# Seven products for eight: Strassen's scheme in the input projection of a short convolution

## The chip, the core and the metric

The kernel runs on one core of a Trainium2 chip. The core has a matrix engine (TensorE, PE in the profile; the loading of its stationary operand is listed apart as PEld), a vector engine (VectorE, DVE), a scalar engine (ScalarE, ACT), GpSimd (POOL) and SyncE (SP), which here issues the transfers between device memory and SBUF, the on-chip memory. PE writes into PSUM, eight banks of 128 x 512 f32. The metric is the device time of one execution in microseconds, as the median of several runs.

## The reference

The model is a trunk of four layers over x (1024 tokens x 1024 channels, f32), with mixers of three kinds: layers 0 and 3 a gated short convolution, layer 1 a diagonal state-space layer, layer 2 an RWKV-7 layer. The change concerns layer 3:

```python
def short_conv_mixer(x, w_in, conv_k, w_out):
    bg, cg, h, z = jnp.split(x @ w_in, 4, axis=-1)
    u = cg * h
    conv = ...                    # width 3 over the tokens, per channel
    return (bg * conv * jax.nn.silu(z)) @ w_out
...
    r = DN_ALPHA * x + y
    r = r + (p[i] @ ple_proj[i]) * jax.nn.sigmoid(r @ ple_gate[i])
    x = layer_norm(r, ln_g[i], ln_b[i])
```

The input projection x @ w_in is 1024 x 1024 x 4096; in the code its four parts have the numbers i = 0 (bg), 1 (cg), 2 (h) and 3 (z).

## The kernel before

Activations lie transposed in SBUF: channels on the 128 partitions, in 8 blocks, tokens along the free dimension in two halves h of 512. For precision every f32 operand is split into a high part, cast by ACT, and a low part, the remainder, subtracted on DVE (`split_into`, L191, for 128 x 512; `wload`, L285 and L286, for a weight block of 128 x 1024, loaded by SP at L282). A product of one output block (128 channels, one half of the tokens) over the 1024 input channels is `mm3`: 8 terms k, each with three matmuls of 512 columns (high x high at L308, high x low at L309, low x high at L310), so 24 matmuls into one PSUM bank.

In the last layer's mixer (`conv_layer`, `unit_both`) the units m = 0 to 7 run over blocks of output channels. Each takes four weight blocks, in the order i = 1, 2, 3, 0, and makes four products per half: cg (copied by ACT), h (u = h x cg, then the three taps of the convolution on DVE), z (its sigmoid on ACT, products on DVE and POOL), and b (the last product, then the split into y). Units 0 and 1 first run for the first half of the tokens, then for the second, with their weights loaded twice, because the second half of x is still being normalised: `ln_gen` of the layer before is a generator, and its pieces are pulled in between the products (counts CP). It takes the mean (`mu`), subtracts it, sums the squares (POOL and DVE), forms 1/sqrt of the variance (`var`, a few small steps on 128 x 4), spreads it (`ln_y`) and scales and splits each block of x (L697, L705, L191). Units 2 to 7 use each weight for both halves. Then `w_out_rows` makes the output product, first for the first half, with the residual alpha x x taken from the high and low parts of x (two DVE steps), and `ple_ln_rows` the gate and the last LayerNorm.

Where buffers lie is set by tags: x in a0 and a1 (by half), y in b0 and b1. Temporaries come from seven slots (`tt`), weights from three buffers each of raw, high and low (wraw, wh, wl), products from four PSUM banks (pmm) and four more (paux). Weights are loaded up to two ahead (AHEAD). The framework orders the instructions of each engine at build time by program order and a model of their durations; on the chip each engine runs its own queue in that order and waits on semaphores.

## Time and profile before

| | |
|---|---|
| three runs | 2869.85, 2872.4, 2874.41 us (median 2872.4) |
| profiled execution | 2874.98 us, its span 2873.3 us |
| PE busy in the span | 2722.6 us (95%), 15131 matmuls |
| DVE, ACT, POOL busy | 1886.0 us (66%), 1121.9 us (39%), 635.8 us (22%) |
| last layer's input products | from 2288.0 to 2648 us |
| its output product | from 2649 to 2737 us |

Numbers of the trace are times from the start of the span. A group is listed by line of the code, engine, operation and tiles (out<-in). Matmuls overlap in their pipeline, so the step from one start to the next, and not the duration of one, tells what they cost. The 40 slices of the page are 71.8 us each.

### The profile page before, as it was taken

What the parts mean: (1) busy time and instruction counts of PE and PEld (TensorE: products, weight loads), DVE (VectorE), ACT (ScalarE), POOL (GpSimd) and SP (SyncE); (2) the same over time, 40 slices, a digit from 0 to 9 for tenths busy, and PEclk for the clock granted to TensorE, in tenths of its full rate; (3) what the DMA queues carried; (4) which work ended last, traced back from release to release, by engine and by line L of the source; (5) the groups of instructions that cost most, each with busy time, mean ns of one, the idle gap of its engine ahead of it and who ended that gap; (6) DMA issues with size and microseconds to landing.
All of it is one profiled execution on the core that took longest, in us unless ns stands there. A gap on an engine that the chain in (4) does not pass through costs nothing.

```text
span 2873.3 us, 40597 instructions
## 1 busy us (share of the span) xinstructions
PE 2722.6 (95%) x15131; PEld 2163.6 (75%) x15131; DVE 1886.0 (66%) x3428; ACT 1121.9 (39%) x2147; POOL 635.8 (22%) x690
## 2 busy tenths in 40 slices
PE   8999999999999999999888799898889999999998
PEld 6877788878877887577666577666667778888887
DVE  6787765477657347878788676887848473333654
ACT  3333322242144223655556465565534231112322
POOL 1243423221207033104333101333232210000000
PEclk9999999999999999999997799997899999999999
DMA  5333322358783333463222254222334332112320
GB/s 166 98 95 96 94 77 62 88 152 225 209 247 124 103 92 119 144 214 96 73 81 89 69 182 141 74 86 83 110 92 143 104 91 59 44 46 64 118 66 37
DMA packets 449749, 312.67 MB, mean 109 GB/s; under 512 B 48360, under 2 KB 393744, under 8 KB 449552
## 3 DMA queue, kind: packets, MB, share of 16 engines
q1 hardware_dynamic: 449552, 310.08, 36.0%
q8 instruction: 119, 1.95, 0.3%
q14 instruction: 78, 0.64, 0.1%
HBM read 240.28 MB, written 69.21 MB: 108 GB/s over the span
## 4 chain that ended last, share of the span: by engine, by line
PE 73%; DVE 14%; ACT 4%; issue 3%; POOL 2%; DMA 2%; SPq 0%; DVEq 0%; POOLq 0%; ACTq 0%
PE op L309 3%; PE op L308 3%; PE op L310 3%; PE gp L310 3%; PE zp L308 3%; PE gp L309 3%; PE zp L309 3%; PE zp L310 3%; PE gp L308 3%; PE sp L308 3%; PE sp L309 3%; PE sp L310 3%; DVE tv L1739 2%; PE hp L308 2%; PE hp L309 2%
## 5 line engine op out<-in xcount | busy, mean ns | idle before, releaser
L286 DVE TENSOR_TENSOR wl<-wraw,wh 128x1024 fp32r<-128x1024 f32 x283 | 365.9, 1294 | 311.5 <-ACT wh L285 303.5
L285 ACT CAST wh<-wraw 128x1024 fp32r<-128x1024 f32 x283 | 296.9, 1050 | 695.5 <-PE gp L309 191.8
L608 POOL TENSOR_TENSOR ln_s<-ln_s,rp 128x512 f32<-128x512 f32 x42 | 60.1, 1430 | 209.8 <-DVE rp L604 209.8
L1825 DVE SCALAR_TENSOR_TENSOR state<-state,pc,p 64x64 f32<-64x64 f32 x256 | 71.0, 277 | 50.1 <-PE p L1822 45.6
L1739 DVE TENSOR_TENSOR tv<-ti,mi 128x128 f32<-128x128 f32 (+3 forms) x128 | 97.1, 759 | 2.4
L1818 PE MATMUL p<-state,ra 128*128 128x128 f32 x256 | 65.7, 344 | 27.3 <-DVE state L1825 25.2
L1819 ACT COPY uv<-p 64x128 f32<-64x128 f32 x128 | 33.2, 259 | 138.8 <-PE p L1818 138.1
L1818 PEld LDWEIGHTS p<-state,ra 128*128 128x128 f32 x256 | 46.3, 219 | 52.7 <-DVE state L1825 42.1
L1673 PEld LDWEIGHTS s<-ra,kb 64*128 64x128 f32 x512 | 64.2, 212 | 20.4 <-ACT scr L1679 6.5
L1673 PE MATMUL s<-ra,kb 64*128 64x128 f32 x512 | 74.7, 314 | 4.4 <-ACT scr L1679 2.1
L1822 PE MATMUL p<-uv,kbt 128*128 128x128 f32 x256 | 67.7, 351 | 10.4 <-ACT uv L1819 10.3
L310 PE MATMUL gp<-r_0h,wl 128*128 128x512 f32 x192 | 76.9, 400 | 0.0
L308 PE MATMUL zp<-x_0h,wh 128*128 128x512 f32 x192 | 76.7, 400 | 0.0
L309 PE MATMUL gp<-r_0l,wh 128*128 128x512 f32 x192 | 76.7, 399 | 0.0
L308 PE MATMUL gp<-r_0h,wh 128*128 128x512 f32 x192 | 76.5, 398 | 0.0
L308 PE MATMUL gp<-r_1h,wh 128*128 128x512 f32 x192 | 76.4, 398 | 0.0
L310 PE MATMUL gp<-r_1h,wl 128*128 128x512 f32 x192 | 76.0, 396 | 0.1
L623 POOL TENSOR_TENSOR rp<-r_0h,r_0l 128x512 f32<-128x512 f32 x24 | 37.4, 1589 | 174.9 <-PE op L309 174.9
L308 PE MATMUL zp<-x_1h,wh 128*128 128x512 f32 x192 | 75.9, 396 | 0.0
L310 PE MATMUL zp<-x_1h,wl 128*128 128x512 f32 x192 | 75.8, 395 | 0.0
L309 PE MATMUL zp<-x_1l,wh 128*128 128x512 f32 x192 | 75.7, 394 | 0.0
L310 PE MATMUL zp<-x_0h,wl 128*128 128x512 f32 x192 | 75.7, 394 | 0.0
(740 smaller groups left out, 8437.6 us busy)
## 6 DMA issues: line engine op xcount, KB each, us to landing
wraw<-in_conv_w_in_dram SPq DMA_DIRECT2D x80, 512.0 KB
wraw<-in_rwkv_w_rkvz_dram SPq DMA_DIRECT2D x64, 512.0 KB
wraw<-in_ple_gate_dram SPq DMA_DIRECT2D x56, 512.0 KB
wraw<-in_conv_w_out_dram SPq DMA_DIRECT2D x24, 512.0 KB
wraw<-in_ssm_w_in_dram SPq DMA_DIRECT2D x21, 512.0 KB
xt<-xd SPq DMA_DIRECT2D x32, 256.0 KB
wraw<-in_rwkv_w_out_dram SPq DMA_DIRECT2D x16, 512.0 KB
wraw<-in_ple_proj_dram SPq DMA_DIRECT2D x14, 512.0 KB
```

The lines of the kernel that those rows point to most:

```text
L285: nc.scalar.copy(wh, raw)
L286: nc.vector.tensor_tensor(wl, raw, f32(wh[:]), ALU.subtract)
L308: nc.tensor.matmul(ps, lh, xh, start=(k == 0), stop=False)
L309: nc.tensor.matmul(ps, lh, xl, start=False, stop=False)
L310: nc.tensor.matmul(ps, ll, xh, start=False, stop=(k == kt - 1))
L608: nc.gpsimd.tensor_tensor(s, s, rs, ALU.add)
L623: (eng or nc.gpsimd).tensor_tensor(rs, f32(rh[:]), f32(rl[:]), ALU.add)
L1673: nc.tensor.matmul(pss[hd][:, c * P:(c + 1) * P], kb[rows, 2 * c + w, :], ra[rows, 2 * c + w, :], start=True, stop=True)
L1739: V.tensor_tensor(tv, ti[:, b:8, 4 * b:4 * b + 4].unsqueeze(2).to_broadcast([P, n, c, 4]), mi[:, 4 * b:4 * b + 4, 0:c].rearrange("p q c -> ...
L1818: nc.tensor.matmul(p1, R.ra[:, c, :], st, start=False, stop=False, skip_group_check=True)
L1822: last = nc.tensor.matmul(p2[:, 0:P], R.kbt[c // 4][:, c % 4, :], uv, start=True, stop=True)
L1825: V.scalar_tensor_tensor(st[cs, cs], st[cs, cs], R.pc[cs, c:c + 1], p2[cs, cs], ALU.mult, ALU.add)
```

## The change

Layer 3's input projection is done by Strassen's scheme in Winograd's form: output channels are taken in pairs of blocks (m, m + 4), tokens in the two halves, input channels in two halves of four blocks. For each of 16 quads (m = 0 to 3, i = 1, 2, 3, 0) seven products q = 1 to 7 of four terms (12 matmuls) take the place of eight. `x_quad` makes sums and differences of the four quarters of x, once for each k, and splits them, inside the generator `ln_gen` after the normalisation of the second half; `w_quad` loads the two weight blocks of a quad and makes and splits the sums of weights (c1, c3 and one in place in r1). Products that several outputs share are added up in PSUM, with DVE or ACT reading the bank in between (s2, s3), and in SBUF by DVE.

For m = 0, 1, 2 the products q1 and q2, which need only the first half of x, are made ahead (12 products, `lead`), while `ln_gen` is pulled (counts QX); q1 is kept in b0, or in memory for m = 2. `tail` puts q4 and q3 of a quad behind q6 of the next. The first tap of the convolution moves from DVE to ACT. Blocks of y with m other than 3 and 7 are stored to memory and loaded again and split before the output product. x in f32 is stored to memory by `ln_gen` and loaded again for the residual, which is then one DVE step. Tags change: y in a0 and b1, sums of x in a1, b0 and b1, r in a1 and a0. The terms of the output product run in the order 0, 1, 2, 4, 5, 6, 3, 7 (ks).

```diff
         for idx, l in enumerate(layers):
             last = idx == len(layers) - 1
             nxt = None if last else layers[idx + 1] % 3
+            S.quads = idx > 0 and (layers[-1] % 3 == 0) and (last or idx == len(layers) - 2)
+            if nxt == 0:
+                S.xf, S.X = [[None, None] for _ in range(NB)], {}
...
     for l in layers:
         kind, j, last = l % 3, l // 3, l == layers[-1]
-        if kind == 0:
+        if kind == 0 and last and l:
+            for m in range(NH):
+                for i in (1, 2, 3, 0):
+                    add("conv_w_in", (j,), i * D + m * P)
+            order.append(None)
+            for _ in range(2):
+                blocks("conv_w_out", (j,))
+            for c in range(2):
+                add("ple_proj", (l,), c * HT, 2, HT)
+        elif kind == 0:
...
+def w_fill(S):
+    while len(S.wready) < min(1 + AHEAD, len(S.worder)) and S.worder[len(S.wready)]:
+        S.wready.append(wload(S, S.worder[len(S.wready)]))
...
 def conv_layer(S, x, l, bg, prep, last):
     nc, A = S.nc, S.A
     region_b(S)
+    if S.quads:
+        return conv_quads(S, x, l, bg)
...
     if last:
-        w_out_rows(S, l, ("conv_w_out", (j,)), y, resid, "a")
+        w_out_rows(S, l, ("conv_w_out", (j,)), y, resid, ("a0", "a1"))
...
+NH = 3
+QX = 1, 2, 2, 3, 3, 2, 3, 3, 3, 3, 3, 3
+def x_quad(S, x, xf, k):
+    V = S.nc.vector
+    x11, x12, x21, x22 = xf[k][0], xf[k][1], xf[k + 4][0], xf[k + 4][1]
+    X = S.X
+    X[3, k] = slot_split(S, "a1", "b22")
+    split_into(S, X[3, k], x22)
+    V.tensor_tensor(x11, x11, x12, ALU.subtract)
+    yield
+    V.tensor_tensor(x12, x22, x12, ALU.subtract)
+    V.scalar_tensor_tensor(x22, x11, -1.0, x22, ALU.mult, ALU.subtract)
+    yield
+    t4 = tt(S, "t4") if k == 3 else x21
+    V.scalar_tensor_tensor(t4, x22, -1.0, x21, ALU.mult, ALU.subtract)
+    for q, t in ((6, x22), (5, x11), (7, x12), (4, t4)):
+        X[q, k] = slot_split(S, ("a1", "b0", "b1", "b1")[k], f"t{q}")
+        split_into(S, X[q, k], t)
+        if q in (5, 4):
+            yield
+def w_quad(S, name, idx, c0, full):
+    nc = S.nc
+    V = nc.vector
+    W = S.A[name][idx].rearrange("(k p) n -> p k n", p=P)
+    r0, r1 = (S.wp.tile([P, NB, P], F32, tag="wraw", name="wraw", bufs=3) for _ in range(2))
+    nc.sync.dma_start(r1, W[:, :, c0 + HT:c0 + HT + P])
+    nc.sync.dma_start(r0, W[:, :, c0:c0 + P])
+    yield
+    q = {}
+    def hilo(src, k=NB):
+        if k == NB:
+            wh, wl = (S.wp.tile([P, k, P], F32R, tag=t, name=t, bufs=3) for t in ("wh", "wl"))
+        else:
+            wh, wl = (S.ws.tile([P, k, P], F32R, tag=t, name=t, bufs=1) for t in ("w3h", "w3l"))
+        nc.scalar.copy(wh, src)
+        V.tensor_tensor(wl, src, f32(wh[:]), ALU.subtract)
+        return wh, wl
+    if full:
+        w = hilo(r0)
+        q[1], q[2] = (*w, 0), (*w, 4)
+        yield
+    c1 = S.ws.tile([P, NB, P], F32, tag="c1", name="c1", bufs=1)
+    V.tensor_tensor(c1[:, 4:8, :], r1[:, 0:4, :], r1[:, 4:8, :], ALU.add)
+    V.tensor_tensor(c1[:, 0:4, :], c1[:, 4:8, :], r0[:, 0:4, :], ALU.add)
+    yield
+    w = hilo(c1)
+    q[6], q[5] = (*w, 0), (*w, 4)
+    yield
+    c3 = S.ws.tile([P, 4, P], F32, tag="c3", name="c3", bufs=1)
+    V.tensor_tensor(c3, r0[:, 0:4, :], r1[:, 0:4, :], ALU.add)
+    V.tensor_tensor(r1[:, 0:4, :], c1[:, 0:4, :], r0[:, 4:8, :], ALU.add)
+    yield
+    w = hilo(c3, 4)
+    q[7] = (*w, 0)
+    yield
+    w = hilo(r1)
+    q[3], q[4] = (*w, 0), (*w, 4)
+    S.wq.append(q)
+    yield
+def conv_quads(S, x, l, bg):
+    nc, A = S.nc, S.A
+    V, G, SC = nc.vector, nc.gpsimd, nc.scalar
+    j = l // 3
+    kw = [S.vec[("conv_k", j, t)] for t in range(3)]
+    X = S.X
+    y = [[None, None] for _ in range(NB)]
+    yd = [S.dram.tile([P, T], F32, tag=f"yd{m}", name=f"yd{m}") for m in range(NB)]
+    s1d = [S.dram.tile([P, HT], F32, tag=f"s1d{i}", name=f"s1d{i}") for i in range(4)]
+    carry, cgs, cvs = {}, {}, {}
+    half = lambda h: slice(h * HT, (h + 1) * HT)
+    st = ExitStack()
+    S.ws = st.enter_context(S.tc.tile_pool(name="ws", bufs=1))
+    S.wq = []
+    tq = lambda nm: S.ws.tile([P, HT], F32, tag="q", name=nm, bufs=4)
+    def mms(ps, w, q, first):
+        wh, wl, k0 = w
+        for k in range(4):
+            xh, xl = X[q, k]
+            nc.tensor.matmul(ps, wh[:, k0 + k, :], xh, start=first and k == 0, stop=False, skip_group_check=True)
+            nc.tensor.matmul(ps, wh[:, k0 + k, :], xl, start=False, stop=False, skip_group_check=True)
+            nc.tensor.matmul(ps, wl[:, k0 + k, :], xh, start=False, stop=k == 3, skip_group_check=True)
+    def block(ps, base=None):
+        if base is None:
+            return ps
+        V.tensor_tensor(base, base, ps, ALU.add)
+        return base
+    def use(i, m, h, v):
+        if i == 1:
+            if v.space == PSUM:
+                t = tq("cg")
+                SC.copy(t, v)
+                v = t
+            cgs[m, h] = v
+        elif i == 2:
+            u = S.tmp.tile([P, HT + 2], F32, tag="t_u", name="u")
+            if h == 0:
+                G.memset(u[:, 0:2], 0.0)
+            else:
+                G.tensor_copy(u[:, 0:2], carry.pop(m))
+            V.tensor_tensor(u[:, 2:], v, cgs.pop((m, h)), ALU.mult)
+            if h == 0:
+                carry[m] = S.tmp.tile([P, 2], F32, tag="t_car", name="car", bufs=4)
+                G.tensor_copy(carry[m], u[:, HT:HT + 2])
+            cv = cvs[m, h] = tt(S, "cv")
+            SC.activation(cv, u[:, 0:HT], AF.Copy, scale=kw[0][:, m:m + 1])
+            V.scalar_tensor_tensor(cv, u[:, 1:HT + 1], kw[1][:, m:m + 1], cv, ALU.mult, ALU.add)
+            V.scalar_tensor_tensor(cv, u[:, 2:HT + 2], kw[2][:, m:m + 1], cv, ALU.mult, ALU.add)
+        elif i == 3:
+            sg = S.tmp.tile([P, HT], F32, tag="ln_v" if h else "ln_s", name="sg", bufs=1) if not bg else tt(S, "sg")
+            SC.activation(sg, v, AF.Sigmoid, scale=1.0 if m < 4 else -1.0)
+            V.tensor_tensor(sg, v, sg, ALU.mult)
+            G.tensor_tensor(cvs[m, h], cvs[m, h], sg, ALU.mult)
+        else:
+            cv = cvs.pop((m, h))
+            V.tensor_tensor(cv, v, cv, ALU.mult)
+            if m % 4 == 3:
+                y[m][h] = slot_split(S, ("a0", "b1")[h], f"y{m}_{h}")
+                split_into(S, y[m][h], cv)
+            else:
+                nc.sync.dma_start(yd[m][:, half(h)], cv)
+    ahead = [(m, i) for m in range(NH) for i in (1, 2, 3, 0)]
+    quads = [(m, i) for m in range(4) for i in (1, 2, 3, 0)]
+    wg = [None] * (len(quads) + 1)
+    def w_begin(p):
+        if p < len(quads):
+            m, i = quads[p]
+            wg[p] = w_quad(S, "conv_w_in", (j,), i * D + m * P, m >= NH)
+            next(wg[p])
+    def w_step(p, n=1):
+        for _ in range(n):
+            if wg[p] is not None and next(wg[p], None) is None:
+                pass
+    s1 = {}
+    for k in range(4):
+        X[1, k], X[2, k] = x[k][0], x[k + 4][0]
+    def lead(n):
+        m, i = ahead[n]
+        w = wprep(S, "conv_w_in", (j,), i * D + m * P)
+        ps = S.pmm.tile([P, HT], F32, tag="mm", name="q1")
+        mms(ps, (*w, 0), 1, True)
+        s = tt(S, "s1d") if m == 2 else slot(S, "b0", "s1")
+        SC.copy(s, ps)
+        if m == 2:
+            nc.sync.dma_start(s1d[n % 4], s)
+        else:
+            s1[m, i] = s
+        return w, ps
+    cur = lead(0)
+    na = len(ahead)
+    for n, (m, i) in enumerate(ahead):
+        nxt = lead(n + 1) if n + 1 < na else None
+        w, ps = cur
+        pull(bg, QX[n])
+        mms(ps, (*w, 4), 2, False)
+        use(i, m, 0, block(ps))
+        cur = nxt
+        if n == na - 5:
+            w_begin(0)
+        if n >= na - 4:
+            w_step(0, 2)
+    while bg:
+        pull(bg)
+    for _ in wg[0]:
+        pass
+    w_begin(1)
+    def tail(st8):
+        (m, i), q, A_, C_, base, s2, v22 = st8
+        mms(A_, q[4], 4, False)
+        use(i, m + 4, 0, block(A_, base))
+        if i == 2:
+            use(i, m + 4, 1, v22)
+        mms(C_, q[3], 3, False)
+        use(i, m, 1, block(C_, s2))
+    def load_y(m, h):
+        t = tt(S, "yl")
+        nc.sync.dma_start(t, yd[m][:, half(h)])
+        y[m][h] = slot_split(S, ("a0", "b1")[h], f"y{m}_{h}")
+        split_into(S, y[m][h], t)
+    prev = None
+    for p, (m, i) in enumerate(quads):
+        q = S.wq.pop(0)
+        final = p == len(quads) - 1
+        if m == 1 and NH == 3:
+            s1[2, i] = slot(S, "b0", "s1")
+            nc.sync.dma_start(s1[2, i], s1d[(1, 2, 3, 0).index(i)])
+        A_ = S.pmm.tile([P, HT], F32, tag="mm", name="qa")
+        if m < NH:
+            base = s1.pop((m, i))
+            mms(A_, q[6], 6, True)
+            s2 = tt(S, "s2")
+            V.tensor_tensor(s2, base, A_, ALU.add)
+            w_step(p + 1, 2)
+            if prev:
+                tail(prev)
+            w_step(p + 1)
+        else:
+            base = None
+            mms(A_, q[1], 1, True)
+            sq = slot(S, "b0", "s1")
+            SC.copy(sq, A_)
+            w_step(p + 1, 2)
+            if prev:
+                tail(prev)
+            D_ = S.paux.tile([P, HT], F32, tag="aux", name="qd")
+            mms(D_, q[2], 2, True)
+            use(i, m, 0, block(D_, sq))
+            w_step(p + 1)
+            if final:
+                for k in (0, 1, 2, 4, 5, 6):
+                    load_y(k, 0)
+            mms(A_, q[6], 6, False)
+            s2 = tt(S, "s2")
+            SC.copy(s2, A_)
+            w_step(p + 1)
+        C_ = S.pmm.tile([P, HT], F32, tag="mm", name="qc")
+        mms(C_, q[5], 5, True)
+        w_step(p + 1)
+        mms(A_, q[7], 7, False)
+        s3 = tq("s3")
+        if base is None:
+            SC.copy(s3, A_)
+        else:
+            V.tensor_tensor(s3, base, A_, ALU.add)
+        block(C_, s3)
+        if i != 2:
+            use(i, m + 4, 1, s3)
+        if wg[p + 1] is not None:
+            for _ in wg[p + 1]:
+                pass
+        w_begin(p + 2)
+        if final:
+            S.worder.pop(0)
+            w_fill(S)
+        prev = (m, i), q, A_, C_, base, s2, s3
+    tail(prev)
+    for k in (0, 1, 2, 4, 5, 6):
+        load_y(k, 1)
+    st.close()
+    region_p(S)
+    def resid(r, m, h, ps):
+        xt = tt(S, "xt")
+        nc.sync.dma_start(xt, x_dram(S)[m][:, half(h)])
+        V.scalar_tensor_tensor(r, xt, ALPHA, ps, ALU.mult, ALU.add)
+    w_out_rows(S, l, ("conv_w_out", (j,)), y, resid, ("a1", "a0"), (0, 1, 2, 4, 5, 6, 3, 7))
...
-    for m in range(NB):
+    quads = nxt == 0 and S.quads
+    for m in (0, 4, 1, 5, 2, 6, 3, 7) if quads and h else range(NB):
         nc.vector.tensor_tensor(rp[m], rp[m], y0, ALU.mult)
         if nxt == 2 and h == 0:
             xf = new_shift(S, m, h, xn)
...
             yield
             continue
         nc.vector.tensor_scalar(rp[m], rp[m], g[:, m:m + 1], b[:, m:m + 1], ALU.mult, ALU.add)
+        if quads:
+            nc.sync.dma_start(x_dram(S)[m][:, h * HT:(h + 1) * HT], rp[m])
+            S.xf[m][h] = rp[m]
+            if h == 0:
+                xn[m][h] = new_split(S, f"x{m}_{h}", "a", h)
+                split_into(S, xn[m][h], rp[m])
+            elif m >= 4:
+                yield
+                yield from x_quad(S, xn, S.xf, m - 4)
+            yield
+            continue
```

More of the change, by code (lines that the diff above doesn't have):

```diff
@@ L292, in wprep, with mm3 @@
     assert S.worder[0] == (name, idx, c0, kt, n), (S.worder[0], name, idx, c0)
-    while len(S.wready) < min(1 + AHEAD, len(S.worder)):
-        S.wready.append(wload(S, S.worder[len(S.wready)]))
+    w_fill(S)
     S.worder.pop(0)
     return S.wready.pop(0)
-def mm3(S, w, rhs, name, ms=0, half=None):
+def w_fill(S):
+    while len(S.wready) < min(1 + AHEAD, len(S.worder)) and S.worder[len(S.wready)]:
+        S.wready.append(wload(S, S.worder[len(S.wready)]))
+def mm3(S, w, rhs, name, ms=0, half=None, ks=None):
     nc = S.nc
@@ L303, in mm3 @@
     kt = len(rhs)
-    for k in range(kt):
+    for n, k in enumerate(ks or range(kt)):
         xh, xl = rhs[k]
@@ L307, in mm3 @@
         ll = wl[:, k, ms:ms + P]
-        nc.tensor.matmul(ps, lh, xh, start=(k == 0), stop=False)
+        nc.tensor.matmul(ps, lh, xh, start=(n == 0), stop=False)
         nc.tensor.matmul(ps, lh, xl, start=False, stop=False)
-        nc.tensor.matmul(ps, ll, xh, start=False, stop=(k == kt - 1))
+        nc.tensor.matmul(ps, ll, xh, start=False, stop=(n == kt - 1))
         if half and k == kt // 2 - 1:
@@ new lines, in conv_quads @@
+def conv_quads(S, x, l, bg):
[171 more added lines that the diff above has]
+            S.worder.pop(0)
+            w_fill(S)
+        prev = (m, i), q, A_, C_, base, s2, s3
[9 more added lines that the diff above has]
+    w_out_rows(S, l, ("conv_w_out", (j,)), y, resid, ("a1", "a0"), (0, 1, 2, 4, 5, 6, 3, 7))
@@ L443, in slot_split, with w_out_unit @@
     return slot(S, tag, name + "h", F32R), slot(S, tag, name + "l", F32R)
-def w_out_unit(S, w, y, resid, tag, m, h):
-    ps = mm3(S, w, [y[k][h] for k in range(NB)], "op")
+def w_out_unit(S, w, y, resid, tag, m, h, ks=None):
+    ps = mm3(S, w, [y[k][h] for k in range(NB)], "op", ks=ks)
     r = tt(S, "r")
@@ L462, in w_out_res, with w_out_rows @@
             w_out_unit(S, w, y, resid, f"{tag}{h}", m, h)
-def w_out_rows(S, l, name, y, resid, tag):
+def w_out_rows(S, l, name, y, resid, tag, ks=None):
     S.r = [[None, None] for _ in range(NB)]
@@ L472, in w_out_rows @@
             w = wprep(S, *name, m * P)
-            w_out_unit(S, w, y, resid, f"{tag}{h}", m, h)
+            w_out_unit(S, w, y, resid, tag[h], m, h, ks)
             if h == 1 and m % 2 == 1:
```

## The prediction

> **What bounds the kernel now.** The page first.
>
> ```profile
> span 2873.3 us, 40597 instructions
> ...
> PE   8999999999999999999888799898889999999998
> ...
> DVE  6787765477657347878788676887848473333654
> ...
> GB/s 166 98 95 96 94 77 62 88 152 225 209 247 124 103 92 119 144 214 96 73 81 89 69 182 141 74 86 83 110 92 143 104 91 59 44 46 64 118 66 37
> ```
>
> Slices 33 to 37 (71.8 us each) are the last mixer's input products: PE stands at 9, DVE at 7 once and then at 3, and the DMA moves 44 to 91 GB/s where another slice reaches 247. The windows of that stage and of the output product behind it:
>
> ```profile
> 2288.00:2648.00 360.00, 359.44 (x1555) 290.47 (x1556) 144.88 (x200) 75.98 (x103) 30.38 (x36) 1.00 0.22 63
> 2649.00:2737.00 88.00, 88.00 (x394) 72.84 (x392) 57.82 (x78) 34.13 (x48) 0.00 (x0) 1.00 0.40 122
> ```
>
> Columns: length, then busy time (count) of PE, PEld, DVE, ACT, POOL, then clock, DMA share, GB/s. PE works for 359.4 of 360 us at full clock; DVE for 145, ACT for 76. The waits of PE in the stage are two:
>
> ```profile
> PE cgp L308 <- DVE sg L603: 1.4, 1, 1.4
> PE cgp L308 <- ACT x_1h L191: 0.6, 1, 0.6
> ```
>
> So the stage lasts as long as its number of matmuls times their pitch. The pitch is the step from start to start, in the timeline of the stage (22 steps between these two)
>
> ```profile
> 2419.83 0.40 PE L309 MATMUL bp<-x_1l,wh 128*128 128x512 f32 x1
> ...
> 2424.95 0.40 PE L310 MATMUL bp<-x_1h,wl 128*128 128x512 f32 x1
> ```
>
> and
>
> ```profile
> 2659.81 0.39 PE L310 MATMUL op<-y_0h,wl 128*128 128x512 f32 x1
> ...
> 2664.79 0.39 PE L308 MATMUL op<-y_0h,wh 128*128 128x512 f32 x1
> ```
>
> 5.12/22 = 0.2327 us in the stage, 4.98/22 = 0.2264 in the output product: 1536 matmuls (64 products of 24) times 0.2327 is 357.4 of the 360 us.
>
> **What it removes.** The scheme makes of each pair of row blocks (m, m+4) one quad: seven products of 12 matmuls where eight stood. 16 quads x 84 = 1344 matmuls, so 192 fewer, 192 x 0.2327 = **44.7 us**. The 0.6 us wait for x_1h goes too, because the first twelve products read the first half of the tokens alone. The pitch may move, as the sums of x lie in other buffers: 4 of 7 products read three of their four terms from b0 and b1, where y lies today. At 0.2264 for these 576 matmuls it would save 3.6 more; the output product, half of which now reads y from a0, could lose 192 x 0.0063 = 1.2. I take nothing for either.
>
> **What it adds on DVE and ACT.** The affine step of LayerNorm among the stage's groups, mean 533 ns:
>
> ```profile
> L705 DVE TENSOR_SCALAR rp<-rp,vec 128x512 f32<-128x512 f32 x8 | 4.1, 533 | 0.0
> ```
>
> In a full queue steps come closer than their durations, which overlap. Three pairs of neighbours in DVE's timeline:
>
> ```profile
> 2286.11 1.23 DVE L286 TENSOR_TENSOR wl<-wraw,wh 128x1024 fp32r<-128x1024 f32 x1 [4.33 <-ACT wh L285]
> 2287.26 0.68 DVE L603 TENSOR_TENSOR sg<-pp,sg 128x512 f32<-128x512 f32 x1
> ```
>
> ```profile
> 2340.16 0.67 DVE L191 TENSOR_TENSOR y_0l<-cv,y_0h 128x512 fp32r<-128x512 f32 x1
> 2340.76 0.67 DVE L191 TENSOR_TENSOR x_1l<-rp,x_1h 128x512 fp32r<-128x512 f32 x1
> ```
>
> ```profile
> 2398.76 0.75 DVE L418 SCALAR_TENSOR_TENSOR cv<-u,vec,cv 128x512 f32<-128x512 f32 x1
> 2399.55 0.75 DVE L419 SCALAR_TENSOR_TENSOR cv<-u,vec,cv 128x512 f32<-128x512 f32 x1
> ```
>
> 1.15 us for 1024 columns and 0.60 for 512, but 0.79 where a step needs the one before it (cv). A quad with m < 3 then costs DVE: four weight sums 2.4, the low parts of the three new weights 2 x 1.15 + 0.60 = 2.9, five additions from PSUM 3.0; and over the four quads of an m nine elementwise blocks of 3 x (0.60 + 2 x 0.75) + 6 x 0.60 = 9.9 (u and the two conv steps; the gate and the last product), so 2.5 each. Sum 10.8 us. PE needs 60 x 0.2327 = 13.9 for it, as two of the seven products were made ahead. With m = 3 it is 2.4 + 4.05 (a fourth weight) + 1.8 (three additions) + 3.9 (four blocks, and splits of y) = 12.2 against 84 x 0.2327 = 19.5. DVE fits, at 78% and 63%, but the i = 2 quads bunch: 8.3 + 6.3 = 14.6 in 13.9. The page has no slice with DVE over 8 tenths, so nothing shows PE fed by so full a DVE. I charge 0.3 us per quad, 5 us (from 0 to 32, the second rival). The last product pair has no next product in front of it and waits for one ACT copy of its PSUM bank, as long as today's of cg:
>
> ```profile
> L403 ACT COPY cg<-cgp x12: 581/585/589, 2386.4 to 2615.5; 128x512 f32<-128x512 f32 x12
> ```
>
> 0.6 and the way there and back, 1 us.
>
> **Beside the path.** The x, y and s1 tiles that go through memory add 64 transfers of 256 KB, and weights of 512 KB are loaded 44 times for 40: some 18 MB over 430 us, 42 GB/s on 63 (and on 122 in the output product). SP issues them all in its queue; a store of y waits there for its DVE product with weight loads behind it, but these are a quad (13.9 us) ahead. In the output product DVE drops one of two residual steps, and xt is loaded before it is needed. Nothing for these, 0 to 3 us if a load is late.
>
> **What it adds on the path: the start.** Today's order of the second half's LayerNorm and of its first use:
>
> ```profile
> 2299.36 0.86 PE mu L663 x2
> ...
> 2316.85 0.90 PE var L685 x8
> ...
> 2323.41 0.89 PE ln_y L692 x8
> ...
> 2338.29 0.51 PE cgp L308
> ```
>
> (from the chain that ended last). After, the mean is asked for behind 24 matmuls (2293.6) instead of 48, but all x sums come behind the LayerNorm: per block k five splits and four sums. What DVE must do from 2294.6 until the sixth operand of k = 3 is there: LayerNorm 20 x 0.60 + 8 x 0.46 (L705, less the overlap of 0.07) + 3.1 (thirteen small steps, below) = 18.8; x sums 33 x 0.62 = 20.5; three m of blocks 3 x 3.3 = 9.8; nine low parts of weights (three are made before) 10.3; the first quad's weights 5.3: 64.7 us. The first and the last of the thirteen:
>
> ```profile
> 2317.79 0.16 DVE L687 TENSOR_SCALAR ln_r<-var 128x4 f32<-128x4 f32 x1 [1.15 <-PE var L685]
> ...
> 2320.86 0.16 DVE L656 SCALAR_TENSOR_TENSOR ln_r<-ln_r,ln_r 128x4 f32<-128x4 f32 x1
> ```
>
> To the 64.7 come 4.5 us of idling before ln_y (nothing else is ready then) and 3 for steps beside POOL (below): 2366.7, and with the cast in front of the last low part 2367.5. PE arrives after 12 x 24 x 0.2327 + 2.65 (mean, var, ln_y) + 9 matmuls = 2359.8 us. **Wait: 8 us**, and behind it in PE's queue stand all quads (0 if DVE idles nowhere and POOL costs nothing, 18 if the LayerNorm chain keeps its old pace). An earlier idle PE of this length shows what follows:
>
> ```profile
> 2124.89 1.12 PE L1860 MATMUL otp<-ident,o 128*128 128x128 f32 x4 [6.79 <-POOL o L1853]
> ```
>
> ```profile
> 2121.00:2129.00 8.00, 4.11 (x13) 3.44 (x14) 4.18 (x10) 1.40 (x2) 4.74 (x5) 0.57 0.23 66
> ```
>
> The granted clock falls to 0.57 over those 8 us: a few microseconds at half rate, 2 us lost. The first quad has no work of another to hide behind: 1.5 us.
>
> POOL's share:
>
> ```profile
> 2308.45 1.19 DVE L678 TENSOR_TENSOR ln_sq<-ln_sq 128x512 f32<-128x512 f32 x1
> ```
>
> ```profile
> 2307.77 3.03 POOL L674 TENSOR_TENSOR ln_v<-ln_v,ln_sq 128x512 f32<-128x512 f32 x2 [3.38 <-ACT ln_sq L672]
> ```
>
> A DVE addition beside POOL takes 1.19 instead of 0.67: 0.5 lost per POOL step, six or seven of them, 3 us. [...] The row (0.5 lost, not 1.5) is below the rule; I go by the row and give the rule 8%, within the forecast's chance.
>
> **Sum**, against the profiled execution (span 2873.3, 2875.0 with what lies around it): -44.7 - 0.6 + 8 + 2 + 1.5 + 5 + 1 = -27.8, so 2847.2. That execution is 2.6 above the median of 2872.4; for a median I say **2845 us**.
>
> **Rivals.**
> *All is hidden* (7%): DVE keeps ahead at the start too and the pitch falls in b0 and b1. Gain 45 to 48, 2826. For it: DVE's sums above are under PE's in every quad. Against: the 64.7 us of DVE work at the start.
>
> *DVE becomes the bound of the quads* (13%): if the steps wait on each other and go at 0.79 instead of 0.60, a quad with m < 3 costs 9 x 0.79 + 3.3 + 3.0 = 13.4 against 13.9 and the i = 2 quads 17.5: some 3.6 us late three times, and the start 4 later. Gain about 13, 2859. Against: most of a quad's DVE steps are sums and low parts of the next quad's weights, and need nothing of the step before.
>
> *Hand-overs, ending slower* (22%): PE adds to one PSUM bank three times, and DVE must read it between q7 and q4 while only 12 matmuls (2.8 us) of the next quad cover that. DVE takes its queue in order; with a low part, a column of blocks and a sum ahead (1.15 + 2.1 + 0.6 + 0.6, then the read 0.6), PE stands for 2.3 us and more. It decides from (44.7 + 0.6 - 12.5)/16 = 2.0 us per quad on; at 3 us the kernel is 15 us slower, 2888. For it, the chain at the present start, where PE's x (its L191 split, then the cgp matmul of 2338.29 above) stands in DVE's queue behind a low part of 2.23 us:
>
> ```profile
> 2332.44 2.23 DVE wl L286
> ```
>
> Against: DVE has 3 us free per quad. A third of this case stays within 0.2%, which is about what a measurement of this kernel can tell from no change.
>
> **Chances.** Forecast (gain 15 to 40 us) 58%, all hidden 7%, DVE bound 13%, hand-overs 22% (15 slower, 7 the same). Faster 78%, same 7%, slower 15%. Range: 2826, the hidden case, to 2874, where stalls eat the gain; beyond lie the slower 15% and a few on the fast side.
>
> **What would show it.** PE matmuls 192 fewer; the stage some 330 us long for 360; a PE wait of 8 us on x sums of k = 3 near 2360 and a half clock behind it; in the quads DVE at 8 or 9 tenths with PE at 9. PE waits on s3 or on the additions over 1 us per quad would show the hand-overs; a DVE without idle time in the quads would show it as the bound; a wait on wraw would show the DMA, which I charge nothing.

## The result, and the profile after

| | before | after |
|---|---|---|
| median of four runs each | 2871.69 us (2869.85 to 2874.41) | 2840.33 us (2832.94 to 2844.80) |
| ratio | | 0.9887, 95% interval 0.9865 to 0.9910 |
| profiled execution | 2874.98 us | 2839.38 us |
| matmuls | 15131 | 14939 |

The forecast was 2845 us in a range of 2826 to 2874. The page of the changed kernel, in the lines that answer to those of before:

```profile
span 2837.7 us, 40655 instructions
...
PE   8999999999999999899888799898889999999998
...
DVE  6787865477657346888888667888756678876544
...
GB/s 168 98 97 97 95 75 66 89 142 212 220 240 140 104 94 122 117 233 107 78 85 87 63 151 170 84 91 89 78 100 135 144 111 111 108 71 129 171 64 38
```

In the slices of the stage (33 to 37) DVE went from 7, 3, 3, 3, 3 to 7, 8, 8, 7, 6, and the transfers from 44 to 91 GB/s to 71 to 129, while PE stayed at 9. "Stage" below is the time from the start of the first product matmul of the last mixer to the start of the last matmul of its output product: before 2287.99 to 2736.65, 448.7 us; after 2285.68 to 2701.10, 415.4 us. So 33.2 of the 35.6 us between the two profiled executions came from the stage. The stage began 2.3 us earlier in this execution, and what follows it took 136.6 us in both.

Four windows of the stage in the changed kernel (columns as before: length, busy time and count of PE, PEld, DVE, ACT, POOL, then clock, DMA share, GB/s): the products made ahead, the hand-over to the quads, steady quads with m < 3, and the m = 3 quads:

```profile
2285.00:2357.00 72.00, 70.13 (x301) 56.38 (x302) 60.90 (x99) 36.34 (x57) 10.34 (x11) 0.98 0.44 134
2357.00:2372.00 15.00, 11.25 (x38) 8.33 (x37) 13.71 (x21) 4.17 (x7) 2.13 (x1) 0.79 0.25 81
2372.00:2527.00 155.00, 155.00 (x669) 125.47 (x668) 128.36 (x175) 42.42 (x53) 21.92 (x22) 1.00 0.33 95
2527.00:2612.00 85.00, 85.00 (x370) 68.96 (x369) 56.32 (x74) 32.32 (x46) 8.38 (x8) 1.00 0.31 97
```

In the quads PE never stands: 155.00 of 155 and 85.00 of 85 us, with DVE at 83% and 66%. Nearly all that was lost lies in the first two windows, where PE misses 1.9 and 3.8 us and the clock is 0.98 and 0.79. The waits of PE in the stage:

```profile
PE qa L506 <- ACT t6h L195: 3.5, 1, 3.5
PE ppt L872 <- DMA praw<-in_p_dram: 1.4, 2, 1.2
PE q L506 <- DVE sg L900: 1.4, 1, 1.4
PE var L982 <- DVE ln_v L979: 0.9, 1, 0.9
```

(sg is the wait at the stage's entry, as before.) The first of them in PE's timeline:

```profile
2362.15 0.39 PE L508 MATMUL qc<-t5h,wl 128*128 128x512 f32 x1
2366.05 0.80 PE L506 MATMUL qa<-t6h,wh 128*128 128x512 f32 x1 [3.52 <-ACT t6h L195]
...
2368.10 0.63 PE L508 MATMUL qa<-t6h,wl 128*128 128x512 f32 x1
2368.53 0.63 PE L506 MATMUL qc<-t5h,wh 128*128 128x512 f32 x1
```

This is the predicted wait, on the sums of x of k = 3, with the half clock behind it: the step from start to start is 0.43 us (2368.10 to 2368.53) where 0.23 is usual. The matmul ahead of the wait belongs to qc, product 5: the order built for PE puts its terms k = 0 to 2, nine matmuls, in front of the last term of product 6.

### The profile page after: what moved, and what is told of

It is laid out like the page before. It is cut to its first block, busy times and chain, and to the rows that moved or that the text cites. A ratio compares the mean times of both kernels' runs of the same rounds, so it can differ in the third digit from the quotient of the medians.

```text
span 2837.7 us, 40655 instructions
## 1 busy us (share of the span) xinstructions
PE 2681.3 (94%) x14939; PEld 2127.4 (75%) x14939; DVE 1994.8 (70%) x3584; ACT 1163.1 (41%) x2211; POOL 646.9 (23%) x696
## 4 chain that ended last, share of the span: by engine, by line
PE 70%; DVE 16%; ACT 4%; issue 4%; DMA 3%; POOL 3%; SPq 0%; DVEq 0%; POOLq 0%; ACTq 0%
PE op L327 3%; PE op L326 3%; PE op L328 3%; PE gp L328 3%; PE gp L327 3%; PE gp L326 3%; PE sp L326 3%; PE sp L327 3%; PE sp L328 2%; DVE tv L2048 2%; PE qa L508 2%; PE qa L506 2%; PE qa L507 2%; PE zp L326 2%; PE zp L328 2%
## 5 line engine op out<-in xcount | busy, mean ns | idle before, releaser
L299 DVE TENSOR_TENSOR wl<-wraw,wh 128x1024 fp32r<-128x1024 f32 x255 | 331.1, 1299 | 217.9 <-ACT wh L298 214.2
L298 ACT CAST wh<-wraw 128x1024 fp32r<-128x1024 f32 x255 | 267.5, 1049 | 517.7 <-PE gp L327 191.5
L1982 PEld LDWEIGHTS s<-ra,kb 64*128 64x128 f32 x512 | 64.7, 213 | 20.4 <-ACT scr L1988 6.2
L327 PE MATMUL gp<-r_1l,wh 128*128 128x512 f32 x192 | 75.6, 394 | 0.0
L2131 PEld LDWEIGHTS p<-uv,kbt 128*128 128x128 f32 x256 | 44.5, 212 | 37.7 <-ACT uv L2128 31.9
L1991 POOL TENSOR_TENSOR scr<-scr,mask 128x512 f32<-128x512 f32 x32 | 46.0, 1436 | 55.4 <-ACT scr L1988 55.2
L326 PE MATMUL sp<-xs0h,wh 128*128 128x512 f32 x128 | 56.1, 438 | 2.6 <-DVE aq L1720 2.2
L327 PE MATMUL sp<-xs0l,wh 128*128 128x512 f32 x128 | 56.0, 437 | 1.9 <-DVE xs0l L195 1.9
```

Of the source, the lines that this page charges most:

```text
L298: nc.scalar.copy(wh, raw)
L299: nc.vector.tensor_tensor(wl, raw, f32(wh[:]), ALU.subtract)
L326: nc.tensor.matmul(ps, lh, xh, start=(n == 0), stop=False)
L327: nc.tensor.matmul(ps, lh, xl, start=False, stop=False)
L1982: nc.tensor.matmul(pss[hd][:, c * P:(c + 1) * P], kb[rows, 2 * c + w, :], ra[rows, 2 * c + w, :], start=True, stop=True)
L2131: last = nc.tensor.matmul(p2[:, 0:P], R.kbt[c // 4][:, c % 4, :], uv, start=True, stop=True)
```

## The experiments

All ratios are to the kernel before, run on the same chip in the same set; the stage is that of each profiled execution.

| run | median us | ratio, 95% interval | stage us | PE waits over 1 us in the stage (sums) |
|---|---|---|---|---|
| changed kernel again | 2835.45 | 0.9872 (0.9855 to 0.9888) | 415.6 | t6h 3.5, praw 1.6 |
| the eighth product | 2875.08 | 1.0014 (1.0005 to 1.0024) | 452.2 | t6h 1.7 |
| four sums more | 2838.66 | 0.9887 (0.9872 to 0.9901) | 415.5 | wh 3.9, s 1.6, praw 1.4 |
| eight sums more | 2865.96 | 0.9967 (0.9954 to 0.9980) | 441.0 | s 19.9, wh 4.1 |
| sums of x first | 2836.08 | 0.9875 (0.9860 to 0.9890) | 414.7 | s 3.8, ln_y 1.0, praw 1.5 |
| eight products ahead | 2851.04 | 0.9922 (0.9898 to 0.9946) | 425.6 | t6h 11.6, praw 1.2 |
| scaling on ACT | 2833.91 | 0.9855 (0.9835 to 0.9874) | 409.1 | praw 1.6 |
| low parts on POOL | 2838.38 | 0.9874 (0.9854 to 0.9894) | 414.5 | t6h 2.1, t6l 1.4, praw 1.2 |
| p loaded later | 2831.88 | 0.9856 (0.9839 to 0.9872) | 407.2 | none |
| variance later | 2831.77 | 0.9856 (0.9837 to 0.9875) | 407.7 | t6h 2.0 |
| order and ACT | 2831.42 | 0.9851 (0.9835 to 0.9866) | 408.0 | ln_y 1.0 |
| nothing ahead of t6 | 2839.79 | 0.9890 (0.9873 to 0.9906) | 417.2 | t6h 5.5 |

**The changed kernel again.** No edit; it shows how far the same kernel repeats.

> The changed kernel once more, as the reference point for the other runs on the same chip. Both theories: about 2840 us, ratio to the kernel before 0.989, one PE wait of 3 to 4 us near 2362 us and a half clock behind it. If the half clock at the start falls differently from run to run, its spread is again wider (2833 to 2845) than that of the kernel before (2870 to 2874).

The median was 4.9 us under that of the first set (2840.33), with intervals that overlap, but the stage was 415.64 against 415.43 us. Its spread (7.9 us in four runs) was not wider than that of the kernel before in this set (10.0 in thirteen). So the verdicts below on a few us go by the stage. These two executions have the same waits within 0.2 us and the same two stretches at half clock; where another kernel has fewer of these stretches, that alone moves its stage by up to 3.7 us. So a difference of 1 or 2 us is read together with the waits and the half clock.

**Is the gain that of the matmuls?** Twelve matmuls more in each of the 16 quads, into a bank that nobody reads:

```diff
+        E_ = S.paux.tile([P, HT], F32, tag="aux", name="qe")
+        mms(E_, q[5], 5, True)
```

> Each of the 16 quads gets an eighth product of 12 matmuls into a free PSUM bank that nobody reads; all else stays. Theory (the quads are bound by PE, and the gain is the 192 matmuls): 192 x 0.2312 = 44 us more, about 2884, no faster than the kernel before. Rival (DVE sets the pace of the quads): the product goes into PE's spare time, 0 to 15 us more, at most 2855.

The whole gain is gone: with eight products for eight the new order is 0.14% slower than the old one (0.05 to 0.24%), some 4 us that sums, start and transfers cost. The stage is 36.8 us longer than the changed kernel's: 192 x 0.2307 (the mean step of this run's input products) = 44.3, less 2.2 us of waits (the start wait is 1.8 shorter) and 3.7 of half clock, which did not come in this run at all. The 1.6 us that are left are small differences of single steps.

**How near is DVE to being the bound?** Sums of x that nobody reads, four and then eight in each quad but the last:

```diff
+        for _ in range(0 if final else 4):
+            dum = S.paux.tile([P, HT], F32, tag="aux", name="dum")
+            V.tensor_tensor(dum, f32(X[1, 0][0][:]), f32(X[1, 1][0][:]), ALU.add)
```

> Each quad but the last gets four more DVE additions of 128x512 into a spare PSUM bank that nobody reads: 15 x 4 x 0.65 = 39 us of DVE work. Theory (DVE needs 10.8 of PE's 13.9 us in the quads of m below 3, 12.2 of 19.5 in those of m = 3): 10.8 + 2.6 = 13.4 still fits, 0 to 6 us more, 2840 to 2846. Rival (DVE is the bound, or PE waits for it at the hand-overs): 30 to 39 us more, 2870 to 2879.

> Each quad but the last gets eight more DVE additions of 128x512 that nobody reads, twice as many as in the run with four. Theory (10.8 of 13.9 us used in the quads of m below 3, 12.2 of 19.5 in the others): 16.0 us per quad no longer fits, 12 quads late by 2.1, about 25 us more than the changed kernel, 2855 to 2868; the quads of m = 3 still fit. Rival (DVE's queue has more room than the sum by steps says): under 10 us more.

The window of steady quads, first with four more:

```profile
2369.00:2524.00 155.00, 153.41 (x662) 123.65 (x661) 152.98 (x222) 42.55 (x53) 19.56 (x21) 1.00 0.31 89
```

then with eight more, and PE's wait there:

```profile
2389.00:2544.00 155.00, 135.61 (x562) 108.15 (x562) 151.44 (x226) 34.49 (x43) 17.79 (x19) 0.96 0.27 78
```

```profile
PE qa L506 <- DVE s L668: 19.9, 8, 5.6
```

A quad of 60 matmuls is 13.9 us, so the 155 us hold 11 quads; the free time of DVE in the changed kernel, 155 - 128.4 = 26.6, is 2.4 us each, four sums of 0.60. Four more fill it (DVE at 152.98 of 155). PE then waits 1.6 us for s in the quads; that the stage stays at 415.5 all the same is because the half clock cost 1.2 us less in this execution. Eight more are 2.4 us over in each, 26 in all; the stage grew by 25.5, of which 19.9 are the waits on s and 4.7 more half clock. PE stood for long only once the sum of DVE's work passed PE's; a DVE that was 99% busy still fed it, but for 1.6 us in 155.

**Is the start wait a matter of DVE's work or of its order?** The first half's uses of the products of m = 2 go behind the sums of x (their products into the other four banks), and the generator's pieces get a higher priority. The amount of work is the same:

```diff
-        use(i, m, 0, block(ps))
+        if n < na - 3:
+            use(i, m, 0, block(ps))
+        else:
+            behind.append((i, m, ps))
...
+    for i, m, ps in behind:
+        use(i, m, 0, block(ps))
```

> The elementwise blocks of the last three products made ahead (m = 2, i = 2, 3, 0) are put behind the sums of x and the first quad's weights in DVE's queue; their products wait in three free PSUM banks. No work is added or left out. Theory (the wait at the first quad is DVE's queue, with a half clock behind it): the wait of 3.5 us and the half clock's 3.7 go, 5 to 8 us less, 2832 to 2835. Rival (the wait is the chain of LayerNorm, mean, variance and scaling, which no order of DVE shortens): within 1 us of 2840.

A miss: the wait at t6h went, and others came in its place.

```profile
PE qa L506 <- DVE s L674: 1.9, 1, 1.9
PE qa L506 <- DVE s L642: 1.9, 1, 1.9
PE ppt L881 <- DMA praw<-in_p_dram: 1.5, 1, 1.5
...
PE ln_y L998 <- DVE ln_r L962: 1.0, 1, 1.0
PE q L508 <- DVE wl L299: 1.0, 1, 1.0
```

L642 and L674 are the first quad's additions s2 and s3, which free the bank for the next product. They now stand in DVE's queue behind what was put off. The stage is 0.7 us shorter, not 5 to 8. PE's waits even add up to more, 8.3 us for 6.4 in the changed kernel, and only a shorter half clock (1.4 us for 3.7) makes up for it. The rival came near in its number but fails as a mechanism, for the order did move the chain: the last cast of t6h ended 73.3 us after the stage's start, 80.3 in the changed kernel. So what DVE owes at the start looks like an amount, and the order chooses who waits for it. The next run takes work away.

**Less work for DVE: scaling on ACT.** The affine step of the second half's LayerNorm (eight steps):

```diff
-        nc.vector.tensor_scalar(rp[m], rp[m], g[:, m:m + 1], b[:, m:m + 1], ALU.mult, ALU.add)
+        if quads and h:
+            nc.scalar.activation(rp[m], rp[m], AF.Identity, scale=g[:, m:m + 1], bias=b[:, m:m + 1])
+        else:
+            nc.vector.tensor_scalar(rp[m], rp[m], g[:, m:m + 1], b[:, m:m + 1], ALU.mult, ALU.add)
```

> The scaling step of the second half's LayerNorm (eight DVE steps of 0.53 us) is done by ACT, which is half idle there; the same work otherwise. Theory after the run that only reordered DVE's queue (its waits moved but did not shrink, so it is the amount of DVE work up to the first quads that is too large): 3.7 to 4 us of DVE work less, so 4 us of PE waits less and some of the half clock, 4 to 7 us less than the changed kernel, about 2830. Rival (the chain through the LayerNorm and the sums of x sets it, and an ACT step in it makes it longer): 0 to 3 us more.

PE's waits in this run's stage:

```profile
PE ppt L872 <- DMA praw<-in_p_dram: 1.6, 2, 1.3
...
PE var L982 <- DVE ln_v L979: 0.9, 1, 0.9
PE qa L506 <- DVE s L633: 0.6, 1, 0.6
```

Eight steps less, 4.8 to 5.3 us of DVE, took away the 3.5 us wait at t6h (0.6 is left, on s) and some 2 of the 3.7 us lost at half clock: the stage is 6.3 us shorter. The last cast of t6h ended 71.8 us after the stage's start, 80.3 in the changed kernel, although a step of ACT now stands in its chain. Together with the run above this shows the cause of the start wait: the amount of DVE's work between the mean and the last sum of x.

**Less work for DVE, but on POOL.** The low parts of two of the four sums of each k go to POOL instead:

```diff
-        split_into(S, X[q, k], t)
+        if q in (7, 4):
+            S.nc.scalar.copy(X[q, k][0], t)
+            S.nc.gpsimd.tensor_tensor(X[q, k][1], t, f32(X[q, k][0][:]), ALU.subtract)
+        else:
+            split_into(S, X[q, k], t)
```

> The low parts of the sums of x for products 7 and 4 (eight DVE steps of 0.60, needed last) go to POOL. By the row that I took for DVE beside POOL (0.5 us lost per POOL step) DVE gains 8 x (0.60 - 0.5), 1 us: 2834 to 2840. [...] If POOL cost DVE nothing: 5 us and some half clock less, 2830.

Nothing is gained to speak of. The stage is 414.5 us, but PE's waits add up to 7.4 us for 6.4; what made it shorter is the half clock behind t6h, 2.1 us in the changed kernel, which did not come here. Groups of DVE at the start (busy, mean ns), first of the changed kernel

```profile
L299 DVE TENSOR_TENSOR wl<-wraw,wh 128x1024 fp32r<-128x1024 f32 x9 | 11.1, 1236 | 1.2 <-ACT wh L298 1.0
...
L1003 DVE TENSOR_SCALAR rp<-rp,vec 128x512 f32<-128x512 f32 x8 | 5.2, 660 | 0.0
...
L975 DVE TENSOR_TENSOR ln_sq<-ln_sq 128x512 f32<-128x512 f32 x3 | 3.6, 1210 | 0.0
L425 DVE TENSOR_TENSOR rp<-rp,rp 128x512 f32<-128x512 f32 x4 | 2.7, 682 | 0.0
...
L465 DVE TENSOR_TENSOR c<-wraw 128x512 f32<-128x512 f32 x2 | 1.4, 679 | 0.0
```

then of this run:

```profile
L299 DVE TENSOR_TENSOR wl<-wraw,wh 128x1024 fp32r<-128x1024 f32 x9 | 11.6, 1284 | 1.1 <-ACT wh L298 1.0
L1007 DVE TENSOR_SCALAR rp<-rp,vec 128x512 f32<-128x512 f32 x8 | 6.2, 793 | 0.0
...
L425 DVE TENSOR_TENSOR rp<-rp,rp 128x512 f32<-128x512 f32 x4 | 3.8, 956 | 0.0
...
L469 DVE TENSOR_TENSOR c<-wraw 128x512 f32<-128x512 f32 x2 | 2.5, 1230 | 0.0
```

The six POOL steps that were there already (ln_v and cv, three each) cost DVE 3 x (1.210 - 0.68) + 8 x (0.660 - 0.533) = 2.6 us, 0.43 each. The six new ones that fall in this stretch cost 8 x 0.133 + 4 x 0.274 + 2 x 0.551 = 3.3 us in the groups of L1007, L425 and L469, and some 0.6 in wl and b22l (1284 for 1236 ns and 734 for 680): 3.9 us, 0.65 each, where each saves 0.60. So a step given to POOL here gave back all of its time on DVE.

These means hide that it is single steps that are drawn out. Two steps of DVE in the changed kernel, and the POOL steps beside them:

```profile
2303.39 1.78 DVE L975 TENSOR_TENSOR ln_sq<-ln_sq 128x512 f32<-128x512 f32 x1
2336.26 1.52 DVE L1003 TENSOR_SCALAR rp<-rp,vec 128x512 f32<-128x512 f32 x1
```

```profile
2302.85 1.77 POOL L971 TENSOR_TENSOR ln_v<-ln_v,ln_sq 128x512 f32<-128x512 f32 x1 [1.18 <-ACT ln_sq L969]
2335.83 1.67 POOL L543 TENSOR_TENSOR cv<-cv,sg 128x512 f32<-128x512 f32 x1 [3.57 <-DVE sg L542]
```

The step of L975 ends 0.55 us after POOL's, that of L1003 0.28 us after. At the start of the stage, eleven DVE steps of 128x512 with two SBUF operands are drawn out like this in the kernel before, the changed one and this run, and all end 0.54 to 0.56 us after a POOL step. So each seems to have waited for POOL's step to end and then to have taken about its own time (0.60 in a full queue). A POOL step cost DVE only what was left of it when such a step came, 1.1 us at most in the changed kernel and nothing where DVE was idle, as at 2311.44: 0.43 us on average, where these POOL steps took 1.5 (ln_v) and 1.7 us (cv) on the mean. Once, at 2359.44, it was POOL's step that was drawn out, to 2.13 us, and the DVE steps beside it kept their length.

**What the third m ahead is worth.** NH = 2, so eight products are made ahead instead of twelve, and eight quads run with m >= NH instead of four:

> Two units (m = 0, 1) instead of three are made ahead: eight products of 24 matmuls in front of the first quad for twelve; m = 2 is done as m = 3 is. The number of matmuls stays. Theory (PE's cover at the start is 4 x 24 x 0.231 = 22 us shorter, DVE has 4 low parts and one unit's blocks less to do there, 7.9 us): 14 us more wait at the first quad and a longer half clock, about 2852. Rival (the start costs what LayerNorm's end costs, and the quads are better fed without units made ahead): within 5 us of 2838.

```diff
-NH = 3
-QX = 1, 2, 2, 3, 3, 2, 3, 3, 3, 3, 3, 3
+NH = 2
+QX = 1, 2, 2, 3, 3, 2, 3, 3
```

```profile
PE qa L506 <- ACT t6h L195: 11.6, 3, 4.2
```

PE reaches the quads sooner by four products of 24 matmuls, and DVE has two thirds of the blocks and weights to do in that time. Three waits of 3.3 to 4.2 us stand where one of 3.5 stood, and the stage is 10.1 us longer. The median is near the 2852 expected, but the wait grew by 8.1 us and not by 14.

**Nothing ahead of t6.** Product 5 of the first quad takes its terms from k = 3 on, so it can't fill the wait:

```diff
-        mms(C_, q[5], 5, True)
+        mms(C_, q[5], 5, True, (3, 0, 1, 2) if p == 0 else (0, 1, 2, 3))
```

> The changed kernel with one edit: product 5 of the first quad takes its terms in the order k = 3, 0, 1, 2, so that none of its matmuls can run before the last sum of x; the work is the same. Theory (the wait at t6h was 3.5 us and not 8 in part because nine matmuls of product 5, 2.1 us, ran ahead of it while PE had nothing else; t6h of k = 3 comes at the same time as before, being set by DVE): a wait on the sums of x of k = 3 of 5 to 6 us, and the stage 2 to 3.5 us longer than the changed kernel's 415.4 to 415.6 (2.1, and what of it falls to the half clock), a median 2 to 3 us above its. Rival (the nine matmuls only fill time that PE loses anyway, since DVE holds the first quads back further on): a longer wait at t6h, but the stage within 1 us of the changed kernel's.

```profile
2357.74 0.39 PE L508 MATMUL qa<-t6h,wl 128*128 128x512 f32 x1
2363.66 0.80 PE L506 MATMUL qa<-t6h,wh 128*128 128x512 f32 x1 [5.53 <-ACT t6h L195]
```

The wait is 2.0 us longer, as nine matmuls are (2.1), and it ends at the same time after the stage's start: 2363.66 - 2283.5 = 80.2 us here, 2366.05 - 2285.7 = 80.4 in the changed kernel. DVE sets this time. The stage is 1.8 us longer, a little under the 2 to 3.5 expected, with 0.6 us less of the wait on praw in it; the median (2839.79) lies inside the spread of the changed kernel's and decides nothing.

**What is left, on top of the scaling on ACT.** First p is loaded four blocks into the output product, instead of at its start:

```diff
-    S.pT = [prep_p(S, l, h) for h in range(2)]
...
+            if h == 0 and m == 4:
+                S.pT = [prep_p(S, l, hh) for hh in range(2)]
```

> The affine steps of the second half on ACT, as in the run of that name, and besides the loads and transposes of p (the ppt matmuls that waited 1.2 us for praw in the output product) are issued after four blocks of the output product instead of at its start. Theory (the wait is for the transfer alone, which was asked for too late behind loads of y and weights): no PE wait on praw, 1.2 to 1.6 us less than with the affine steps on ACT alone, a ratio near 0.985 to before, some 2832 us. Rival (the transfer only moves its lateness to another load that shares the queue, or the transposes now hold up the gate behind the output product): a wait of 1 us or more on another DMA or on pT, and the time within 1 us of that run.

The wait on praw is gone, nothing takes its place, and the stage is 2.0 us shorter than with the scaling alone. Then, on top of this, the piece that asks for var is pulled one product later (QX = 1, 2, 1, 4, 3, ...):

> As the run with p loaded later, and the piece of the generator that asks for var on PE is pulled one product (12 matmuls, 2.8 us) later, with the pieces behind it made up at the next product. Theory (PE takes its queue in order, and stands 0.95 us for ln_v only because var is asked for before DVE has summed the squares; the half clock behind it, 1.8 us, comes from that stand): the PE wait on ln_v is gone and so is the half clock near 2308, 1.5 to 2.5 us less in the stage. Rival (DVE is what the stage start waits for: with var later DVE idles 1 to 2.8 us longer before ln_y, and the wait comes back in front of the products with t6h or on s): the stage is as long or up to 2 us longer.

The rival held. The wait for ln_v and the half clock behind it went, and the same came back at the quads:

```profile
PE qa L506 <- ACT t6h L195: 2.0, 1, 2.0
```

The stage is 0.6 us longer. Last, the order of the run with the sums of x first, with scaling on ACT and p later:

> The affine steps of the second half on ACT and p loaded later, and besides the first half's uses of the products of m = 2 behind the sums of x, as in the run with the sums of x first. Theory (at the start the amount of DVE work decides, and after 8 steps fewer the work that is left fits under PE's lead in either order): stage within 2 us of the run with p loaded later, no wait at t6h, waits of DVE s of at most 2 us in all. Rival (the order still costs or gains): 3 us or more to either side, through waits on s in the first two quads (longer) or a start without any wait (shorter).

The stage stayed within 1 us (408.0 for 407.2), but not because nothing changed: PE's waits add up to 3.5 us for 1.8, and the half clock behind the wait for ln_v, 1.4 us in the other run, did not come. So this run does not show that the order is free once the work fits; it bounds its price at some 2 us. The last three runs and the scaling on ACT alone can't be told apart by their whole times (2831 to 2834 us); they are the fastest here, 1.4 to 1.5% under the kernel before.

## Why the prediction was right

The mechanism held: PE bounds the stage, the gain is 192 matmuls, and the price is a start in which DVE is late. The sizes, term by term against the profiled executions:

| term | predicted us | measured us |
|---|---|---|
| 192 matmuls less | -44.7 | -44.5 |
| pitch of the input products | 0, down to -3.6 | -0.9 |
| x_1h | -0.6 | -0.6 |
| start wait on k = 3 | +8 | +3.5 |
| half clock | +2 | +3.7 |
| first quad | +1.5 | 0 |
| hand-overs in steady quads | +5 | 0 |
| last hand-over | +1 | 0 |
| waits on ln_v, s1d, wh and praw | 0 | +2.8 |
| pitch of the output product | 0, up to 1.2 | +0.9 |
| sum | -27.8 | -35.1 |

The stage shrank by 33.2. Most of the 1.9 us between is at the edges of the waits: the last matmul in front of each of the six waits holds PE for its 0.39 us or more, and not for a step of 0.23 (1.2 us), and the edges of the stretches at half clock take 0.4.

- **Matmuls.** 192 x 0.2320, the mean step of the input products before, outside waits; in the changed kernel it is 0.2313. In a stretch of the quads it is (2424.84 - 2419.73)/22 = 0.2323, between these two:

```profile
2419.73 0.39 PE L507 MATMUL qa<-t4l,wh 128*128 128x512 f32 x1
...
2424.84 0.39 PE L508 MATMUL qc<-t5h,wl 128*128 128x512 f32 x1
```

- **The start wait** was mis-sized by 4.5 us, on PE's side and not on DVE's. From the mean to the sixth operand the prediction gave DVE 2367.5 - 2294.6 = 72.9 us; measured are 2366.05 - 2292.41 = 73.6 (DVE was busy for 66.4 of them, where 64.7 and 3 beside POOL were added up, and idle for 7.2, where 4.5 were), from this step on:

```profile
2292.41 0.69 DVE L964 TENSOR_TENSOR rp<-rp,mu 128x512 f32<-128x512 f32 x1 [5.06 <-PE mu L960]
```

PE, however, arrived later. Less the 2.3 us by which the stage began earlier, the prediction has it there at 2357.5, and it came at 2362.5. Of these 5.0 us nine matmuls of product 5 are 2.1 (the prediction let quads run in the order of the code; the run with nothing ahead of t6 shows them), the stand for ln_v 0.95, the half clock behind that 1.6, and s1d 0.2.

- **The half clock** lay in two places, of 2.1 us behind t6h, as predicted (2), and of 1.6. The second was not foreseen: it lies behind a stand of under 1 us.

```profile
2305.15 0.39 PE L508 MATMUL q<-x_0h,wl 128*128 128x512 f32 x1
2306.49 1.05 PE L982 MATMUL var<-mean_w,ln_v 128*128 128x1 f32 x8 [0.95 <-DVE ln_v L979]
...
2308.15 0.63 PE L508 MATMUL q<-x_0h,wl 128*128 128x512 f32 x1
2308.57 0.63 PE L506 MATMUL q<-x_0h,wh 128*128 128x512 f32 x1
```

Nineteen matmuls in all ran at 0.426 instead of 0.231 us: 3.7 us.
- **Quads.** The charge of 0.3 us per quad was for a DVE that is too full at 78% in an even load. It was 83% busy and PE never stood; in the sums runs the loss began only near 100% (1.6 us of 155 at 99%). The bunch of the i = 2 quads (14.6 in 13.9) cost nothing here. With eight sums more the longest waits (5.6, 4.9 and 4.9 us) stand before product 4 of the i = 3 quads, the ones behind i = 2, as the bunch would have it; the two of 0.7 and 0.9 with four sums more stand one quad later, at i = 0 of m = 0 and 1. So the second rival (DVE as the bound) needs 2.4 us more per quad than there were. The third (2 us of stand per quad) is near what eight sums more look like.
- **First and last quad.** The first had the second quad's product 6 and its own product 5 to fill it. The last was covered by the first terms of the output product, which the order built for PE runs ahead: op starts 11 us before the last qc.
- **POOL.** The price of 0.5 us per POOL step held (0.43 measured over six), and the sum of 3 us too (2.6). No run shows the 1.5 us lost per POOL step to which the prediction gives its 8%: single steps were drawn out, by 1.1 us at most in the changed kernel. The low part of 2.23 us that the third rival took as a sign is such a step too: POOL's step beside it ended at 2333.59, and the low part 1.08 us later.
- **Charged at nothing.** No PE wait names the transfers of y, s1 or the weights, but the loads of y hold up another. SP's timeline of the changed kernel:

```profile
2605.43 8.81 SPq L617 DMA_DIRECT2D yl<-yd  x6
2615.06 0.38 SPq L295 DMA_DIRECT2D wraw<-in_conv_w_out_dram  x1
2615.66 0.93 SPq L866 DMA_DIRECT2D praw<-in_p_dram  x2
```

  praw is asked for behind six loads of y, 5 us before its use at 2620; before, its first loads went out at 2629.9, 19 us ahead of the output product. The prediction looked in this queue at y, the weights and xt, and not at p; its 0 to 3 us for a late load cover the 1.4. They went when p was loaded later.

So the errors of size partly cancel, which is luck: 4.5 us too much for the start wait, 7.5 for the quads and hand-overs, against 1.7 too little for the half clock and 2.8 for the other waits. What is left made the forecast 4.7 us high, well inside its range (7.8 us against the profiled execution, 2.3 of which lie ahead of the stage).

## What to carry to other kernels

Where one engine is full and another has room, add up the second engine's work against the first's stretch by stretch: until the sum passes it next to nothing was lost here (0 at 83%, 1.6 of 155 us at 99%), and past it all of the excess (25.5 us of 26). The cost then sits where the sum is over, here at the start of the stage. Taking work away helped; another order moved the wait to someone else. When you work out a wait, ask too what the instruction scheduler can put in front of it on the waiting engine.

## What the runs showed of the hardware

- The granted clock was 0.50 behind a stand of 0.95 us and eight matmuls of one column (0.9 us), and again at the wait of 3.5 us:

```profile
2307.70:2311.11 3.41, 3.41 (x9) 2.65 (x8) 3.10 (x14) 1.54 (x2) 0.00 (x0) 0.50 0.00 0
2365.73:2372.55 6.82, 6.26 (x14) 4.60 (x15) 6.16 (x10) 3.76 (x6) 0.00 (x0) 0.50 0.05 12
```

  Of the twelve kernels with the stand of 0.95 us, eight had this stretch behind it (seven or eight matmuls, 1.4 to 1.6 us lost) and four had none: the eighth product, sums of x first, eight products ahead, order and ACT. The loss does not follow the length of the stand either: 2.1 us behind 3.5, 2.0 behind 5.5, 1.2 behind 3.9 (four sums more), none behind 1.7 (the eighth product). The two stretches lasted 3.41 and 6.82 us. These runs do not show what sets these lengths, nor what decides between the eight and the four.
- The step of the output product's first half grew from 0.2269 to 0.2315 us when its y moved from b0 to a0. In the second half, with y in b1 in both kernels, it stayed at 0.2267. Whether the place or the denser transfers (181 GB/s in the window of the output product, 122 before) make the difference was not tried.
